# A two-layer streaming encoder on one core: S5 angle multiples from one sine and cosine routine, gate constants ahead of the S5 table, expert gathers at first sizes

## The chip, the cores and the metric

The kernel runs on one core of a Trainium2 chip. The metric is device time in microseconds (us) for one execution. TensorE (PE) multiplies, VectorE (DVE), ScalarE (ACT) and GpSimd (POOL) work on the results, and SyncE (SP) issues most transfers. Each engine runs its own instructions in order and waits on semaphores for the others.

## What is computed

512 frames of 1024 channels go through two layers. Each layer has a token mixer with three branches (chunked attention, RG-LRU, S5) and a channel mixer: a dense SwiGLU in layer 0, eight experts with two chosen per token in layer 1. Cut to what the change touches:

```python
def _rglru_branch(xr, gate, conv_w, conv_b, wx, bx, wa, ba, lam):
    ...
    log_a = -RG_C * ga * jax.nn.softplus(-lam.astype(jnp.float32))
    ...

def _s5_branch(u, a_re, a_im, log_dt, b_re, b_im, c_re, c_im, d, w_glu):
    A = lax.complex(a_re.astype(jnp.float32), a_im.astype(jnp.float32))
    dt = jnp.exp(log_dt.astype(jnp.float32))[:, None]
    A_bar = jnp.exp(A * dt)
    B_bar = ((A_bar - 1.0) / A)[..., None] * Bm
    ...
    states = _linear_scan(A_seq, Bu)

def _moe(x2, router, w1, w3, w2):
    logits = x2.astype(jnp.float32) @ router.astype(jnp.float32)
    top_logit, top_e = lax.top_k(logits, TOP_K)
    ...
    yb = lax.map(expert_block, (xb, blk_e)).reshape(n_pad, dm)
```

## The kernel before

All matrix weights are float32 and are split into two float16 parts (`wh` on ScalarE, `wl` on VectorE, lines L219 and L232); each product is three matmuls (L592 to L594). A unit of weights is 512 KB; it is issued by SyncE into one of eight raw buffers, four units ahead.

**Layer 0, mixer (0 to about 260 us).** The order of the mixer's pieces is a string, `ORDER`, one per layer, written out by hand; each piece issues its instructions on all engines in that order. The pieces that matter: `x.8` and `x.10` are the small S5 parameters (`small_params`, `small_params1`: exponentials, sine and cosine, the factors of B), `x.11` is `a0` (powers of A_bar and B_bar on POOL), `x.13` is `a3` (the table E of 64 powers of A_bar's eighth power, in six doublings, and the radius table R), `x.12` is `rg_params` (the constants of the RG-LRU gates, a softplus of lambda; it ends by writing rgh, L447). All of these run on POOL, one after the other. POOL's list is fed by no planner; it is the order of the string. `small_params` works on both layers at once (16 columns, 8 per layer). Sine and cosine come from `vsincos`; `small_params2` doubles the angle three times by products, and `a3` doubles it five times more in the tile rot.

`ke.0` is the key tile of head pair 0 (kh on ScalarE L1031, kl on VectorE L1033), `z.0` and `z.1` are the RG-LRU gates: `tg` on ScalarE (L698) reads four PSUM banks and rgh, then VectorE continues in tg (L710, L714) with ga (L703) and the scan (L722). `S.0`, `S.1`, ... are the attention scores of one query block (TensorE L866 and L867, then VectorE `sc`, L868, with the running maximum mx, and `nm`, L874); `E.0`, ... the exponentials on ScalarE (L881). PSUM has eight banks. The tiles of S5 and attention share rotating buffers, so a score tile can have to wait until a POOL tile that had its buffer is written or read.

**Dense FFN (to about 640 us).** 22 steps f of 128 hidden columns. A dictionary `z1` hangs layer 1's S5 preparation on single steps: `Z1.steps` (a0, a1, a2, a3, a2s, a4, ...) at f = 1, 2, 3, 4, 8, 9, 11, 12, 14 and `consts` at 18.

**Experts (845 us to the end).** The eight experts are sorted by load and run in four pairs. For each pair and each of up to nine variants in `VARS[p]` (column counts of the two experts) the program holds an arm; a control value read from the router's counts takes one by a chain of branches (`choose`, L1739). Before a pair, `gathers(p, d)` for d = 0 to 7 collects the experts' tokens as products with one-hot matrices (TensorE L1355, 8 matmuls per expert and d), and ScalarE and VectorE write them as float16 parts xg (L1356, L1357). The size of a gather is `TOP`, the largest of the variants: (328, 72), (272, 120), (232, 128), (176, 160). Pair 0's d = 0 to 3 run before the control values are there. Pair 2's gathers stand in two halves around a loop `over` (L1760, L1761) that handles tokens beyond the variants' sizes. In an arm come 22 up steps f of both experts, then eight down steps dt, whose results are copied (`yt`, L1384) and written by `back` (y, L1393). `announce` marks where each engine is told of a coming branch; it stands just ahead of a pair's gathers, and for the loop ahead of pair 2's first half.

## Time and profile before

| | us |
|---|---|
| median of 3 runs | 1708.54 |
| lowest, highest | 1705.78, 1710.72 |
| profiled execution | 1702.69 |
| its span, first to last instruction | 1701.0 |
| TensorE busy in the span | 1606.1 (94%) |
| VectorE busy | 1218.7 (72%) |
| ScalarE busy | 997.1 (59%) |
| POOL busy | 443.2 (26%) |

The mean granted clock of TensorE in the span is 0.965 of its full speed. Shares over the whole span mix stages with different limits, so the table of stretches and the timelines below are read stage by stage. In a timeline, "idle before" is the time in which the engine stood still just before that row, and the name behind the arrow is what ended it.

### The profile page before, as it was taken

What the parts mean: (1) busy time and instruction counts of PE and PEld (TensorE: products, weight loads), DVE (VectorE), ACT (ScalarE), POOL (GpSimd) and SP (SyncE); (2) the same over time, 40 slices, a digit from 0 to 9 for tenths busy, and PEclk for the clock granted to TensorE, in tenths of its full rate; (3) what the DMA queues carried; (4) which work ended last, traced back from release to release, by engine and by line L of the source; (5) the groups of instructions that cost most, each with busy time, mean ns of one, the idle gap of its engine ahead of it and who ended that gap; (6) DMA issues with size and microseconds to landing.
All of it is one profiled execution on the core that took longest, in us unless ns stands there. A gap on an engine that the chain in (4) does not pass through costs nothing. (4 is left out here: it accounts for less than half of the span.)

```text
span 1701.0 us, 44318 instructions
## 1 busy us (share of the span) xinstructions
PE 1606.1 (94%) x18058; PEld 1206.7 (71%) x18058; DVE 1218.7 (72%) x1732; ACT 997.1 (59%) x1643; POOL 443.2 (26%) x643
## 2 busy tenths in 40 slices
PE   8959999999999999899889999999989999999995
PEld 4425555445444444455489999899989999989985
DVE  5856664643342245847779988799978998799987
ACT  5444543232331234645477876788867887678874
POOL 6972015930000000300213321233102331023411
PEclk9978899999999999789899999999999999999998
DMA  7312336322332324210089999799997999899994
GB/s 273 111 38 65 100 100 225 101 98 100 114 125 98 124 69 137 63 50 14 10 320 339 351 341 352 263 381 372 386 360 268 379 363 375 301 328 393 378 383 166
DMA packets 123601, 374.56 MB, mean 220 GB/s; under 512 B 30129, under 2 KB 30321, under 8 KB 123362
## 3 DMA queue, kind: packets, MB, share of 16 engines
q1 hardware_dynamic: 96626, 343.00, 55.0%
q10 hardware_dynamic: 21568, 14.24, 2.8%
q0 software_dynamic: 5168, 14.17, 2.3%
q8 instruction: 146, 2.39, 0.6%
q14 instruction: 93, 0.76, 0.1%
HBM read 356.04 MB, written 14.12 MB: 218 GB/s over the span
## 5 line engine op out<-in xcount | busy, mean ns | idle before, releaser
L594 PEld LDWEIGHTS <-wl 128*128 128x128 f16 x4816 | 463.3, 98 | 96.5 <-DVE wl L232 25.6
L232 DVE SCALAR_TENSOR_TENSOR wl<-raw,wh 128x1024 f16<-128x1024 f32 (+1 forms) x374 | 468.6, 1281 | 76.6 <-PE ps L598 51.4
L592 PEld LDWEIGHTS <-wh 128*128 128x128 f16 x4816 | 463.8, 98 | 69.1 <-issue 4.3
L593 PEld LDWEIGHTS <-wh 128*128 128x128 f16 x4816 | 463.1, 98 | 67.1 <-issue 1.6
L594 PE MATMUL ps<-xg,wl 128*128 128x232 f16 (+7 forms) x2816 | 483.1, 222 | 8.9 <-DVE wl L232 8.4
L592 PE MATMUL ps<-xg,wh 128*128 128x232 f16 (+7 forms) x2816 | 482.9, 222 | 1.4 <-ACT xg L1356 1.1
L593 PE MATMUL ps<-xg,wh 128*128 128x232 f16 (+7 forms) x2816 | 483.5, 222 | 0.0
L219 ACT ACTIVATE wh<-raw 128x1024 f16<-128x1024 f32 (+1 forms) x374 | 376.0, 1031 | 137.3 <-PE ps L599 74.2
L298 POOL TENSOR_TENSOR gbuf<-sg,gbuf 128x232 f16<-128x232 f32 (+7 forms) x176 | 180.1, 1023 | 393.0 <-ACT gbuf L1371 393.0
L594 PE MATMUL ps<-gbuf,wl 128*128 128x232 f16 (+7 forms) x1408 | 246.1, 223 | 10.2 <-DVE wl L232 10.1
L592 PE MATMUL ps<-gbuf,wh 128*128 128x232 f16 (+7 forms) x1408 | 246.4, 223 | 0.0
L593 PE MATMUL ps<-gbuf,wh 128*128 128x232 f16 (+7 forms) x1408 | 246.3, 223 | 0.0
L593 PE MATMUL ps<-fl,wh 128*128 128x512 f16 (+1 forms) x368 | 136.1, 370 | 0.7 <-DVE fl L603 0.7
L592 PE MATMUL ps<-fh,wh 128*128 128x512 f16 (+1 forms) x368 | 136.1, 370 | 0.4 <-ACT fh L602 0.4
L594 PE MATMUL ps<-fh,wl 128*128 128x512 f16 (+1 forms) x368 | 136.1, 370 | 0.0
L1371 ACT ACTIVATE gbuf<-sg 128x232 f16<-128x232 f32 (+7 forms) x176 | 55.4, 315 | 80.7 <-DVE sg L1370 80.7
L286 POOL TENSOR_SCALAR rv<-ss 128x1 f32<-128x1 f32 x24 | 5.1, 214 | 348.1 <-ACT u L609 290.8
L232 DVE SCALAR_TENSOR_TENSOR wl<-raw4m,wh 128x1024 f16<-128x1024 f32 (+1 forms) x68 | 94.8, 1395 | 0.1
L1165 DVE SCALAR_TENSOR_TENSOR slu<-ps,slu 128x512 f32<-128x512 f32 x22 | 15.2, 692 | 109.3 <-PE ps L594 98.4
L232 DVE SCALAR_TENSOR_TENSOR wl<-raw6m,wh 128x1024 f16<-128x1024 f32 (+1 forms) x68 | 87.6, 1289 | 1.8 <-ACT wh L219 1.8
L592 PE MATMUL ps<-uh,wh 128*128 128x512 f16 x224 | 86.5, 386 | 0.0
L593 PE MATMUL ps<-ul,wh 128*128 128x512 f16 x224 | 86.3, 385 | 0.0
(407 smaller groups left out, 2771.8 us busy)
## 6 DMA issues: line engine op xcount, KB each, us to landing
raw<-mw SPq DMA_DIRECT2D x240, 512.0 KB
raw<-fw SPq DMA_DIRECT2D x66, 512.0 KB
raw6m<-mw SPq DMA_DIRECT2D x60, 512.0 KB
raw7m<-mw SPq DMA_DIRECT2D x60, 512.0 KB
raw4m<-mw SPq DMA_DIRECT2D x60, 512.0 KB
raw5m<-mw SPq DMA_DIRECT2D x60, 512.0 KB
raw<-win SPq DMA_DIRECT2D x36, 512.0 KB
raw<-mw SPq DMA_DIRECT2D x32, 384.0 KB
```

Source lines behind the costliest of these rows:

```text
L219: A.activation(whs[u % WH_BUFS][:, :units[u][2]], w_raw(u), AF.Copy, scale=WS)
L232: V.scalar_tensor_tensor(lo, w_raw(u), WS, h, op0=OP.mult, op1=OP.subtract)
L286: P.tensor_scalar(v, ss, inv, EPS, op0=OP.mult, op1=OP.add)
L298: (e or V).tensor_tensor(o, x, y, op=OP.subtract)
L592: T.matmul(ps, wh, xh, start=start, stop=False)
L593: T.matmul(ps, wh, xl, start=False, stop=False)
L594: T.matmul(ps, wl, xh, start=False, stop=stop)
L1165: V.scalar_tensor_tensor(sl, pp[1], OUT_S * GS, sl, op0=OP.mult, op1=OP.mult)
L1371: A.activation(gh[:, f], sg[:, 1, :N], AF.Copy)
```

## The change

Three things. (1) `vsincos` is written anew: it takes the angles as they are, reduces them by whole turns, evaluates the series at a quarter of the angle and doubles twice. It is called once per layer with seven multiples of each angle (1, 8, 16, ..., 256 times; tile `ang`), 8 x 7 = 56 columns, so the doublings in `small_params2` and in rot go; `a3` reads its factors from `ang`. Parameters are per layer: layer 0's in `x.8` and `x.10`, layer 1's at f = 1 and 2 of the dense FFN, and layer 1's preparation starts at f = 3. (2) In layer 0's order `x.12` stands ahead of `x.13`. (3) Gathers ahead of a pair use `VARS[p][0]`, the first variant's sizes; an arm with a larger variant gathers the rest itself (`more`), and the first variant's arm has nothing to add. Pair 2's gathers all come after the loop `over`. The announcements for the loop and for the arms of pairs 1 and 3 move into the pair before, behind down step dt = KD - 3 = 5.

```diff
-    "v.2.0 x.13 A.3 x.12 v.2.1 Ae.3 v.3.0 wb v.3.1 vt.2 vt.3 v.2.2 v.3.2 v.2.3 ve.2 wc v.3.3 v.0.2 v.1.2 v.0.3 v.1.3 ve.3 "
+    "v.2.0 x.12 x.13 A.3 v.2.1 Ae.3 v.3.0 wb v.3.1 vt.2 vt.3 v.2.2 v.3.2 v.2.3 ve.2 wc v.3.3 v.0.2 v.1.2 v.0.3 v.1.3 ve.3 "
...
+    def vsincos(sc, y, n):
+
+        tmp = sm(3 * n, name="sct", bufs=1).rearrange("p (i n) -> p i n", i=3)
+        k, r, t = (tmp[:, i] for i in range(3))
+        P.tensor_scalar(k, y, 0.5 / math.pi, RND, op0=OP.mult, op1=OP.add)
         P.tensor_scalar(k, k, RND, None, op0=OP.subtract)
...
+        for i, c in enumerate((6.28125, 1.9350051879882812e-3, 3.0199159795e-7)):
+            P.tensor_scalar(t, k, -c, None, op0=OP.mult)
+            add(r, t, r if i else y, P)
+        mul(t, r, r, P)
+        r2 = t.unsqueeze(1).to_broadcast([128, 2, n])
+        co = lambda i: srs[:, i].unsqueeze(2).to_broadcast([128, 2, n])
+        mul(sc, r2, co(0), P)
+        for i in range(1, 6):
+            add(sc, sc, co(i), P)
+            if i < 5:
+                mul(sc, sc, r2, P)
         s, c = sc[:, 0], sc[:, 1]
         mul(s, s, r, P)
...
+        for _ in range(2):
+            mul(t, s, s, P)
+            mul(s, s, c, P)
+            add(s, s, s, P)
+            P.tensor_scalar(c, t, -2.0, 1.0, op0=OP.mult, op1=OP.add)
...
-    def small_params2():
         mul(r8, ex, ex, P)
         mul(r8, r8, r8, P)
         mul(r8, r8, r8, P)
-        c, s = cs, sn
-        for i in range(3):
...
         def a3(e=P):
-            if l == 0:
-                small_params2()
...
-            rot = t2([128, 7, 2, 8], name="rot")
-            P.tensor_copy(rot[:, 0, 0], c8[:, j])
-            P.tensor_copy(rot[:, 0, 1], s8[:, j])
-            for i in range(5):
...
             for i in range(6):
                 m = 1 << i
-                br = rot[:, i, 0].unsqueeze(2).to_broadcast([128, 8, m])
-                bi = rot[:, i, 1].unsqueeze(2).to_broadcast([128, 8, m])
+                br = ang[:, 2, i + 1].unsqueeze(2).to_broadcast([128, 8, m])
+                bi = ang[:, 1, i + 1].unsqueeze(2).to_broadcast([128, 8, m])
...
-    z1 = dict(zip((1, 2, 3, 4, 8, 9, 11, 12, 14, 18), Z1.steps + [consts]))
-    z1[2] = lambda: Z1.steps[1](P)
+    z1 = dict(zip((3, 4, 5, 6, 9, 10, 11, 12, 14, 18), Z1.steps + [consts]))
+    z1[1], z1[2] = lambda: small_params(1), lambda: small_params1(1)
+    z1[4] = lambda: Z1.steps[1](P)
...
-        for i in range(2):
-            n = TOP[i * NP_ + p]
-            Expert(n, xgv(p, i, n), None).gather(d, ohv(p, i), low)
+
+        for i, n in enumerate(VARS[p][0]):
+            Expert(n, xgv(p, i, n), None).gather(d, ohv(p, i)[:, :, :n], low)
+
+    def more(p, n):
+
+        for d in range(KD):
+            for i, m in enumerate(VARS[p][0]):
+                if n[i] > m:
+                    x = [t[:, :, m:] for t in xgv(p, i, n[i])]
+                    Expert(n[i] - m, x, None).gather(d, ohv(p, i)[:, :, m:n[i]])
...
+            if dt == KD - 3:
+                announce(None if p == 1 else p + 1)
         back(*last)
...
         if p == 2:
-            announce(n_over > 0, "over")
-            d0 = 4
-            for d in range(d0):
-                gathers(p, d)
             with tc.If(n_over > 0, label="over"):
                 with tc.For_i(0, n_over, 1) as it:
                     beyond(it)
-        announce(ctls[p] > 0, f"pair{p}_0")
-        for d in range(d0, KD):
+        if p % 2 == 0:
+            announce(p)
+        for d in range(4 if p == 0 else 0, KD):
             gathers(p, d, A.copy if p == 0 and d < 6 else V.tensor_copy)
```

The order of instructions, at three places. First POOL in layer 0's mixer, from the end of `a0` (bz) on; pc holds the S5 parameters, Et is scratch of the table E, rgp the gate parameters. Before:

```order
L490 COPY bz<-bb 64x16x16
L292 TENSOR_TENSOR pc<-pc 128x16 [waits Pool_49] x3
L292 TENSOR_TENSOR tv_408<-pc 128x16
...
L423 TENSOR_SCALAR pc<-tv_420 128x16
L521 MEMSET E 128x8
...
L525 COPY rot<-pc 128x8 [waits Pool_49]
...
L292 TENSOR_TENSOR rot<-rot 128x8 [waits Pool_49]
...
L292 TENSOR_TENSOR Et<-E,rot 128x8 x2
...
L540 COPY R<-pc 128x8x63
L431 TENSOR_SCALAR tv_501<-rgp 128x4 [waits DMAHW1_49]
...
L447 TENSOR_SCALAR rgh<-rgp 128x8
```

and now:

```order
L472 COPY bz<-bb 64x16x16
L414 TENSOR_SCALAR tv_387<-rgp 128x4 [waits DMAHW1_49,Pool_49]
...
L326 TENSOR_TENSOR tv_389<-pcn,tv_388 128x4 [waits Pool_49]
...
L429 TENSOR_SCALAR sp_154<-tv_402 128x4
L430 TENSOR_SCALAR rgh<-rgp 128x8
L501 MEMSET E 128x8
...
L292 TENSOR_TENSOR Et<-E,ang 128x8 [waits Pool_49] x2
L298 TENSOR_TENSOR E<-Et 128x8 [waits Pool_49]
...
L512 COPY R<-pc 128x8x63
```

The operations on rgp up to rgh now stand ahead of E, and the products on pc and rot between bz and E are gone.

Second, VectorE from `ke.0` to the gates, where wl is a weight split. Before:

```order
L232 SCALAR_TENSOR_TENSOR wl_116<-raw_104,wh_112 128x1024
L1033 SCALAR_TENSOR_TENSOR kl<-ps,kh 64x512 [waits PE_49,Activation_49,Pool_49]
...
L1035 COPY kh<-kh 64x512 x2
L859 MEMSET bias 64x2x64
L868 ISA sc,mx<-ps,bias 128x128 [waits DVE_49,PE_49,Pool_49]
...
L874 TENSOR_SCALAR nm<-mx 128x2 [waits DVE_49]
L710 SCALAR_TENSOR_TENSOR tg<-tg,xc 128x1024 [waits DMAHW1_49,Activation_49]
L868 ISA sc,mx<-ps,bias 128x256 [waits PE_49]
```

and now:

```order
L232 SCALAR_TENSOR_TENSOR wl_116<-raw_104,wh_112 128x1024
L1005 SCALAR_TENSOR_TENSOR kl<-ps,kh 64x512 [waits PE_49,Activation_49]
...
L1007 COPY kh<-kh 64x512 x2
L831 MEMSET bias 64x2x64
L840 ISA sc,mx<-ps,bias 128x128 [waits DVE_49,PE_49,Pool_49]
...
L846 TENSOR_SCALAR nm<-mx 128x2 [waits DVE_49]
L682 SCALAR_TENSOR_TENSOR tg<-tg,xc 128x1024 [waits DMAHW1_49,Activation_49]
L840 ISA sc,mx<-ps,bias 128x256 [waits PE_49]
```

The order is the same; kl has lost its wait for POOL, the first `sc` keeps one.

Third, ScalarE between pair 1 (yt 128x80 is its last down step's copy) and pair 2 (xg are the gathers). Before:

```order
L219 ACTIVATE wh_108<-raw_100 128x1024 [waits DMAHW7_49,DVE_49]
L1384 ACTIVATE yt<-ps 128x80 [waits PE_49,Activation_49]
L1739 UNCONDITIONAL_BRANCH
...
L1853 BRANCH_PREFETCH_HINT
L1356 ACTIVATE xg_7470<-ps 128x232 [waits PE_49]
L1356 ACTIVATE xg_7470<-ps 128x128 [waits PE_49]
...
L1760 COMPARE_AND_BRANCH
L1761 COMPARE_AND_BRANCH
...
L1853 BRANCH_PREFETCH_HINT
```

and now:

```order
L1834 BRANCH_PREFETCH_HINT
L219 ACTIVATE wh_113<-raw7m 128x768 [waits DMAHW4_49,DVE_49]
...
L1358 ACTIVATE yt<-ps 128x176 [waits PE_49,Activation_49]
...
L1358 ACTIVATE yt<-ps 128x80 [waits PE_49,Activation_49]
L1729 UNCONDITIONAL_BRANCH
L1740 COMPARE_AND_BRANCH
L1741 COMPARE_AND_BRANCH
...
L1834 BRANCH_PREFETCH_HINT
L1330 ACTIVATE xg_7442<-ps 128x160 [waits PE_49]
L1330 ACTIVATE xg_7442<-ps 128x112 [waits PE_49]
```

The hint for the loop (the first BRANCH_PREFETCH_HINT) has moved from behind the arm's last copy to ahead of its last four; the loop's branches (L1760 and L1761, now L1740 and L1741) come before any gather, and the hint for pair 2's arm stands, as before, ahead of gathers, now of all eight.

## Rows read from the trace of the kernel before

**Rows 1.** Stretches, in us: length, busy per engine, granted clock, DMA share, GB/s

```profile
92.00:130.00 38.00, 20.27 (x169) 9.82 (x168) 20.03 (x40) 18.87 (x37) 26.93 (x48) 0.69 0.10 32
...
270.00:500.00 230.00, 230.00 (x1133) 108.99 (x1132) 100.94 (x102) 73.76 (x98) 71.72 (x116) 1.00 0.37 125
...
862.00:1063.00 201.00, 198.00 (x3108) 194.89 (x3107) 178.94 (x214) 152.16 (x237) 51.58 (x50) 1.00 0.93 338
...
1265.00:1290.00 25.00, 20.55 (x265) 19.74 (x266) 11.22 (x25) 9.70 (x24) 2.34 (x3) 0.93 0.37 138
```

**Rows 2.** Instruction groups by form on TensorE: count, busy us, mean ns, idle

```profile
L592 PE MATMUL ps<-xg,wh 128*128 128x232 f16 x352 | 92.4, 262 | 1.1 <-ACT xg L1356 1.1
```

**Rows 3.** Timeline of ScalarE, front: start, length, operation, count, [idle <- releaser]

```profile
92.02 1.19 ACT L1031 ACTIVATE kh<-ps 64x512 f16<-64x512 f32 x2
...
110.19 2.42 ACT L698 ACTIVATE tg<-ps,rgh 128x512 f32<-128x512 f32 x4 [16.98 <-POOL rgh L447]
...
115.35 0.39 ACT L881 ACTIVATE sc<-sc,nm 128x128 f32<-128x128 f32 x1
```

**Rows 4.** Timeline of VectorE, same stretch, columns as above

```profile
98.36 1.39 DVE L1033 SCALAR_TENSOR_TENSOR kl<-ps,kh 64x512 f16<-64x512 f32 x2 [4.52 <-POOL Et L292]
...
100.76 0.29 DVE L868 CUSTOM_DVE_ANT_0 sc<-ps,bias 128x128 f32<-128x128 f32 x1 [0.24 <-POOL tv L298]
...
101.43 0.17 DVE L874 TENSOR_SCALAR nm<-mx 128x2 f32<-128x2 f32 x1
...
111.49 1.22 DVE L710 SCALAR_TENSOR_TENSOR tg<-tg,xc 128x1024 f32<-128x1024 f32 x1 [9.89 <-ACT tg L698]
...
117.73 1.23 DVE L714 SCALAR_TENSOR_TENSOR tg<-xc,tg 128x1024 f32<-128x1024 f32 x1 [2.97 <-ACT tg L707]
```

**Rows 5.** Timeline of TensorE, same stretch

```profile
100.12 0.29 PE L866 MATMUL ps<-kh,q 128*128 128x128 f16 x1 [8.04 <-DVE kh L1035]
...
110.93 0.37 PE L866 MATMUL ps<-kh,q 128*128 128x256 f16 x1 [9.22 <-ACT tg L698]
```

**Rows 6.** Timeline of POOL, 17 to 112 us

```profile
18.67 2.91 POOL L326 TENSOR_TENSOR pc<-pcn,tv 128x16 f32<-128x16 f32 x1
...
56.05 3.58 POOL L292 TENSOR_TENSOR pc<-pc 128x16 f32<-128x16 f32 x3
...
62.12 0.21 POOL L295 TENSOR_TENSOR tv<-tv 128x16 f32<-128x16 f32 x1
...
76.83 1.64 POOL L292 TENSOR_TENSOR Et<-E,rot 128x8 f32<-128x8 f32 x2
...
98.41 0.72 POOL L295 TENSOR_TENSOR E<-Et 128x256 f32<-128x256 f32 x1
...
99.69 0.23 POOL L431 TENSOR_SCALAR tv<-rgp 128x4 f32<-128x4 f32 x1
...
109.92 0.24 POOL L447 TENSOR_SCALAR rgh<-rgp 128x8 f32<-128x8 f32 x1
```

**Rows 7.** Timeline of TensorE: the gathers (L1355) ahead of pairs 0 to 3

```profile
854.35 5.66 PE L1355 MATMUL ps<-ohb,raw 128*128 128x328 f16 x64 [1.34 <-ACT xg L1357]
...
1068.73 10.95 PE L1355 MATMUL ps<-ohb,raw 128*128 128x272 f16 x128
...
1265.68 5.12 PE L1355 MATMUL ps<-ohb,raw 128*128 128x232 f16 x64 [0.32 <-DVE y L1393]
...
1274.88 6.78 PE L1355 MATMUL ps<-ohb,raw 128*128 128x232 f16 x64 [4.07 <-DVEq L1760]
...
1472.10 9.45 PE L1355 MATMUL ps<-ohb,raw 128*128 128x176 f16 x128
```

**Rows 8.** Timeline of ScalarE: the first weight split in pairs 1 to 3

```profile
1082.40 1.06 ACT L219 ACTIVATE wh<-raw 128x1024 f16<-128x1024 f32 x1 [2.41 <-DVE wl L232]
...
1284.40 1.06 ACT L219 ACTIVATE wh<-raw 128x1024 f16<-128x1024 f32 x1 [2.42 <-issue]
...
1484.65 1.06 ACT L219 ACTIVATE wh<-raw 128x1024 f16<-128x1024 f32 x1 [2.77 <-issue]
```

More of the change, by code (lines that the diff above doesn't have):

```diff
@@ L329, in vrcp @@
         P.tensor_tensor(o, x, pcn[:, 2, 0:n], op=OP.pow)
[L331 to L356 removed]
+    q4 = lambda k: (-1.0) ** (k // 2) / math.factorial(k) / 4.0 ** k
@@ new lines, in tile_trunk @@
+    SERIES = [(q4(11 - 2 * i), q4(10 - 2 * i)) for i in range(6)]
+    NM = 7
+    srs = cpool.tile([128, 6, 2], F32, name="srs")
+    mults = cpool.tile([128, NM], F32, name="mults")
+    for i, c in enumerate(SERIES):
+        for k in range(2):
+            P.memset(srs[:, i, k:k + 1], c[k])
+    for i in range(NM):
+        P.memset(mults[:, i:i + 1], 2.0 ** (i + 2 if i else 0))
+    ang = cpool.tile([128, 3, NM, 8], F32, name="ang")
+    def vsincos(sc, y, n):
+        tmp = sm(3 * n, name="sct", bufs=1).rearrange("p (i n) -> p i n", i=3)
+        k, r, t = (tmp[:, i] for i in range(3))
+        P.tensor_scalar(k, y, 0.5 / math.pi, RND, op0=OP.mult, op1=OP.add)
+        P.tensor_scalar(k, k, RND, None, op0=OP.subtract)
+        for i, c in enumerate((6.28125, 1.9350051879882812e-3, 3.0199159795e-7)):
[9 more added lines that the diff above has]
+                mul(sc, sc, r2, P)
@@ L371, in vsincos @@
-        mul(t2_, c, sn_, P)
-        add(so, t1, t2_, P)
-        mul(t1, c, cm, P)
-        mul(t2_, s, sn_, P)
-        sub(co, t1, t2_, P)
-    NP = 16
+        for _ in range(2):
[3 more added lines that the diff above has]
+            P.tensor_scalar(c, t, -2.0, 1.0, op0=OP.mult, op1=OP.add)
     are, aim, ldt = s5p[:, 0], s5p[:, 1], s5p[:, 2]
-    pc = cpool.tile([128, 16, NP], F32, name="pc")
-    dt_, ex, sn, cs, a_re, a_im, f_re, f_im, r8, c8, s8 = (pc[:, i] for i in range(11))
+    pc = cpool.tile([128, 8, 8], F32, name="pc")
@@ L382, in tile_trunk, with small_params @@
+    dt_, ex, a_re, a_im, f_re, f_im, r8, xr = (pc[:, i] for i in range(8))
     sp4 = cpool.tile([128, 2, 2, 2], F32, name="sp4")
     rgh = cpool.tile([128, 2, 2, 2], F32, name="rgh")
-    sp_xr, sp_yi = tv(NP), tv(NP)
-    def small_params():
-        vexp(dt_, ldt, NP)
-        mul(sp_xr, are, dt_, P)
-        mul(sp_yi, aim, dt_, P)
-    def small_params1():
-        vexp(ex, sp_xr, NP)
-        vsincos(sn, cs, sp_yi, NP)
-        mul(a_re, ex, cs, P)
-        mul(a_im, ex, sn, P)
-        m1, t1, t2_, den = tv(NP), tv(NP), tv(NP), tv(NP)
+    def small_params(l=0):
+        j = slice(8 * l, 8 * l + 8)
+        vexp(dt_, ldt[:, j], 8)
+        mul(xr, are[:, j], dt_, P)
+        mul(ang[:, 0, 0], aim[:, j], dt_, P)
+        mul(ang[:, 0, 1:], ang[:, 0, 0:1].to_broadcast([128, NM - 1, 8]), mults[:, 1:].unsqueeze(2).to_broadcast([128, NM - 1, 8]), P)
@@ L398, in small_params1 @@
+    def small_params1(l=0):
+        j = slice(8 * l, 8 * l + 8)
+        re, im = are[:, j], aim[:, j]
+        vexp(ex, xr, 8)
+        vsincos(ang[:, 1:3].rearrange("p i m j -> p i (m j)"), ang[:, 0].rearrange("p m j -> p (m j)"), 8 * NM)
+        mul(a_re, ex, ang[:, 2, 0], P)
+        mul(a_im, ex, ang[:, 1, 0], P)
+        m1, t1, t2_, den = tv(8), tv(8), tv(8), tv(8)
         P.tensor_scalar(m1, a_re, -1.0, None, op0=OP.add)
-        mul(t1, are, are, P)
-        mul(t2_, aim, aim, P)
+        mul(t1, re, re, P)
+        mul(t2_, im, im, P)
@@ L1698, in pair_last, with announce @@
             SY.dma_start(out[b * 128:(b + 1) * 128], of[b])
+    def announce(p):
+        label, c = ("over", n_over) if p is None else (f"pair{p}_0", ctls[p])
+        tc.mark_branch_hint_location(label, c > 0, mybir.ALL_ENGINES)
     def pair(p, v):
@@ L1708, in pair @@
             ex.append(Expert(n[i], xgv(p, i, n[i]), g))
+        more(p, n)
         if p == NP_ - 1:
```

73 lines of the change are left out of this document (10 added, 63 removed).

## The prediction

> **What bounds the kernel now.** I read the table of stretches first [rows 1]. Between 270 and 500 us TensorE is busy for all 230.00 us, so what is added there on other engines costs nothing while it stays beside it. Between 92 and 130 us TensorE works 20.27 of 38.00 us at a granted clock of 0.69: the front of layer 0 waits. From 862 us on the experts run with TensorE busy 198.00 of 201.00 us and the DMA share at 0.93, but in the passage from pair 1 to pair 2 (1265 to 1290 us) that share is 0.37 and VectorE works 11.22 of 25.00 us. So two places have slack in which a shorter chain is a shorter program: the front and the passages between pairs. The forms of the up matmuls [rows 2] name the variant taken: 352 matmuls at 232 columns are pair 0's smallest variant, (232, 56), and the other forms (56, 176, 80, 160, 112, 136, 120) are the first variants of the other three. The gathers, however, run at the largest sizes (328 and 72 for pair 0).
>
> Then the three timelines of the front. ScalarE, done with kh at 93.21, stands 16.98 us until POOL's rgh, and runs `tg` at 110.19 [rows 3]. POOL ends rgh at 110.16, after the rotation table E (last write 98.41 + 0.72 = 99.13) and after the 34 operations of the gate constants from 99.69 on [rows 6]. VectorE and TensorE stand behind ScalarE: the first tg on VectorE is at 111.49 after 9.89 us idle [rows 4], the second pair of S matmuls at 110.93 after 9.22 us, since `tg` holds the banks [rows 5]. Before that VectorE's kl waited 4.52 us for a late read of POOL's scratch tile Et [rows 4].
>
> **The change, part 1: the front.** It moves the gate constants (x.12) ahead of the table (x.13), removes the doubling chain of `small_params2` (12 operations) and the rotation chain (22), and computes sine and cosine of seven angle multiples at once, on 8 columns per layer: operations of 56 and 112 columns instead of 16 and 32. The rows of the order show that kl loses its POOL wait, that S.0's first `sc` on VectorE keeps one (the write of E ends just ahead of it in the trace, and I take that to be it), and that `tg` waits only for rgh.
>
> POOL's new chain: its exponentials start at 18.67 as before. The 128x16 form took 2.91 us [rows 6]; on 8 columns I estimate 1.7. Replaying the new list with the durations of the old rows, and letting an operation that starts beside a VectorE operation on SBUF last until that ends (the three products at 56.05 took 1.19 each, the sum at 62.12 took 0.21 [rows 6]), a0 ends at about 55.8 as now, since more columns per operation eat what fewer operations save. The 34 operations of the constants then fall into the stretch where VectorE is busiest: about 23 us instead of the 10.5 of 99.69 to 110.16. So rgh comes at about 79 (77 to 82) instead of 110.16, 14 us before ScalarE can use it. E starts at about 79, 2 us later than today's first product of it (76.83 [rows 6]); of that the replay gives back some, as fewer of its operations lie beside VectorE's, and E ends at about 99, as now (97 to 102).
>
> What is late next: ScalarE runs `tg` at 93.2, 17 us earlier. VectorE does kl right after its weight split, near 94, and then S.0's `sc` waits for the end of E, about 99, instead of 100.76. From the `sc` row to the tg row behind it lie four short rows, the last of which ends at 101.60 [rows 4], 0.84 us in all, so tg comes at 99.85 instead of 111.49: 11.6 us. The 2.97 us that VectorE idles at 117.73 for ScalarE [rows 4] go as well, since ScalarE's `sc` of 115.35 [rows 3] then stands 15 us earlier and the sigmoid behind it no longer ends last; then the gain is up to 14.6. The U matmuls, in order behind S.3, set which of the two counts. I take 13. Bounds: 9.6 (E at 101, no more) to 16 (E at 97, and a clock that falls less, 0.69 in this stretch [rows 1]). Behind it the layer's order is a fixed chain on three engines, and it passes the gain on.
>
> Layer 1's parameters move into the dense FFN, some 24 us of POOL operations in its steps 1 and 2, and layer 1's preparation two steps later. TensorE is the bound there [rows 1]; POOL has 71.72 of 230.00 us in use and VectorE 100.94. Nothing, and below nothing there is no reason. If this cover were gone it would be at most those 24 us.
>
> **Part 2: the gathers.** Columns per d and term fall: 400 to 288, 392 to 256, 360 to 272, 336 to 256. A d has 8 passes over these columns. The passage from pair 0 to 1 took 10.95 us for 8 x 8 x 392 columns, 0.44 ns each [rows 7], and the others lie within 2% of that.
> - Pair 0: only d 4 to 7 stand on the path (5.66 us; d 0 to 3 end before a wait that ends later). 4 x 8 x 288 columns take 4.05: 1.6 us.
> - Pair 1: 8 x 8 x 256 columns take 7.15 instead of 10.95: 3.8 us.
> - Pair 3: 7.15 instead of 9.45: 2.3 us.
> - Pair 2: today 5.12 us of gathers, 4.07 idle until VectorE has its branch, 6.78 for the other half (1.66 more than the first; the stretch's granted clock is 0.93 [rows 1], and I put the difference down to a clock that fell after the idle), and ScalarE's split at 1284.40, 2.74 later [rows 7, 8]: 18.7 in all. After the change the branch comes first: 4.07 + 7.7 (272 columns) + 1.66 + 2.74 = 16.2, a gain of 2.5. If the idle shortens because the branch was announced two down steps earlier, or the clock holds, it is up to 8. I take 4.
>
> Together 11.7. It isn't eaten by the weights' transfer: a passage leaves DMA idle (0.37 of 25 us [rows 1]) because the raw buffers are full; a passage that ends earlier starts the queue earlier.
>
> The announcements for pairs 1 and 3 and for the overflow loop move behind the third down step from the end. Before, with the announcement ahead of the whole gather, ScalarE's first split in the arm still came after 2.41, 2.42 and 2.77 us of idle [rows 8]. ScalarE's announcement for pair 1 stood some 11 us ahead of the branch and the 2.41 came all the same, so I expect nothing from more distance: 0, with 2.5 us per passage either way.
> The Trainium skill, "Runtime: NRT & Kernel Launch", section "Instruction fetch mechanics", says that prefetch is sequential over two pages of 256 instructions, and that a taken branch to a target outside them stalls for a fetch. By it an announcement made hundreds of TensorE instructions ahead could be thrown out again before the branch; the sum would then lose the first rival's price. No row of before shows an announcement that far ahead.
>
> **The sum.** 13 + 1.6 + 3.8 + 4 + 2.3 = 24.7 us. The profiled execution took 1702.69 (span 1701.0), which would become 1678.0. It lies 5.85 us under the median of the runs, 1708.54, so the predicted median is 1683.8, say 1684. A measurement of this kernel can tell about 0.3%, 5 us, from no change.
>
> **The rivals.**
> 1. *The early announcement is lost.* Three branches (pair 1, overflow, pair 3) then pay a fetch that today is announced: 2.77 (ScalarE's longest start) to 4.07 us (TensorE's wait for VectorE at a branch) each, 8 to 12 in all: 1692 to 1696. For it: between announcement and branch now lie two down steps of both experts and the jump at the arm's end, where before there was one gather. Against it: after a passage TensorE stands about 2.7 us ahead of ScalarE's split anyway [rows 7, 8], so TensorE's own fetch would partly hide, and ScalarE's start was no better with the announcement close by. Chance 0.14.
> 2. *E comes late and gates S.0.* If all 34 operations of the constants took 1.19 us, as those at 56.05, they would last 40 us and not 23, E would end at 115, tg on VectorE at 116: 4.5 us lost instead of 13 won, 1701. Halfway, E at 107, the front gains 3.5: 1693. Against it: not every operation there is stretched (0.21 at 62.12 [rows 6]), and VectorE's work on SBUF ends near 94, before kl. Chance 0.12.
> 3. *The weights set the experts' time.* With a DMA share of 0.93 the savings of part 2 would be given back in the next pair: 1708.5 - 13 = 1695. Against it: the idle DMA of each passage. Chance 0.06.
> 4. *Slower: announcements fetch twice.* At the same three places an early announcement costs a stall where its page comes in and another fetch at the branch. At 4.07 each, twice three times, 24 us are lost and the change is worth nothing; above that it is slower, and by over 0.3% from 5 us each, 30 in all: 1714. It would need more than the longest such wait in the trace, which a DMA queue near its limit (0.93) could cause. Chance 0.03.
> 5. *Better:* the announced branches save 2.5 us at three passages, or the front brings 16: 1668 to 1675. Chance 0.03.
>
> **How the numbers follow.** The forecast has 0.62, on its own 1676 to 1691. The range that leaves out no more than 2 in 10 takes in the first three rivals' middles: 1674 to 1699. Faster by over 0.3%, under 1703.4: the forecast, rivals 1, 2, 3 and 5, less a little of 2's far end: 0.93. Within 0.3%: 0.04. Slower: 0.03.
>
> **What would show it.** In the front: rgh near 79, `tg` on ScalarE near 93, no POOL wait ahead of kl, S.0's `sc` right behind the last write of E near 99, tg on VectorE near 100. In the passages: gathers of pairs 1 and 3 near 7.2 us and ScalarE's first split 2.4 to 2.8 us after the last eviction; pair 2's gathers in one piece behind the overflow branch. The dense FFN as long as before. Wrong would be: E after 103, idle TensorE inside a down step of pairs 0, 1 or 2, or a pair that takes longer from its first split to its last than before.

## The result

The changed kernel takes 1688.53 us (median of 4 runs, 1683.74 to 1691.41) against 1709.63 for the kernel before: a ratio of 0.9893, 95% interval 0.9870 to 0.9916. In a second comparison on another chip it was 1689.89 against 1705.35, 0.9903 (0.9880 to 0.9926). So the gain is 16.5 to 18.3 us by the ratios (15.5 and 21.1 by the medians, whose quotients differ a little from the ratios), where 24.7 was forecast. The time lies 4.5 us above the predicted 1684, inside the range.

The front in the changed kernel first. Columns of a timeline: start, length, engine and line, operation, tiles, count, idle time before and what ended it. POOL:

```profile
79.59 0.74 POOL L430 TENSOR_SCALAR rgh<-rgp 128x8 f32<-128x8 f32 x1
...
102.17 1.89 POOL L292 TENSOR_TENSOR xc<-ga 128x1024 f32<-128x1024 f32 x1 [1.47 <-DVE tg L682]
104.00 3.54 POOL L550 MEMSET wt<- 128x2048 f16 x2
```

ScalarE and VectorE:

```profile
92.56 2.42 ACT L670 ACTIVATE tg<-ps,rgh 128x512 f32<-128x512 f32 x4
...
107.87 0.62 ACT L853 ACTIVATE sc<-sc,nm 128x384 f32<-128x384 f32 x1 [4.62 <-DVE nm L846]
```

```profile
93.04 1.39 DVE L1005 SCALAR_TENSOR_TENSOR kl<-ps,kh 64x512 f16<-64x512 f32 x2
...
100.15 0.29 DVE L840 CUSTOM_DVE_ANT_0 sc<-ps,bias 128x128 f32<-128x128 f32 x1 [4.82 <-POOL E L295]
...
100.77 1.23 DVE L682 SCALAR_TENSOR_TENSOR tg<-tg,xc 128x1024 f32<-128x1024 f32 x1
...
102.72 4.85 DVE L846 TENSOR_SCALAR nm<-mx 128x2 f32<-128x2 f32 x1
104.00 3.57 DVE L840 CUSTOM_DVE_ANT_0 sc<-ps,bias 128x384 f32<-128x384 f32 x1
...
110.30 2.48 DVE L292 TENSOR_TENSOR dm<-ps,E 128x512 f32<-128x512 f32 x4
```

Four things stand in these rows. rgh ends at 80.33 and no longer holds `tg`, which starts at 92.56 [against rows 3]. kl has no wait [rows 4]. The first score waits 4.82 us for the table E, as forecast. And a wait that was not forecast stands behind them: nm, an operation on 256 numbers, lasts 4.85 us, and the score behind it 3.57; both end at 107.57, with POOL's zeroing of `wt`.

The experts, in stretches cut at the same events in both kernels: first gather, first up result (`sg`) of a pair, last copy (`yt`) of its down steps. Columns: stretch, length, busy time (instructions) of PE, PEld, DVE, ACT and POOL, granted clock, DMA share, GB/s. The changed kernel, into pair 0, 0 to 1, 1 to 2, 2 to 3, and pair 3 with its DMA share of 0.90:

```profile
834.87:856.09 21.22, 16.56 (x178) 14.54 (x178) 10.64 (x47) 12.75 (x36) 0.00 (x0) 0.85 0.69 253
...
1056.38:1069.25 12.87, 12.57 (x214) 12.29 (x215) 6.80 (x21) 6.33 (x20) 1.86 (x2) 1.00 0.52 196
...
1249.66:1268.51 18.85, 13.18 (x184) 12.93 (x185) 7.54 (x21) 6.76 (x20) 1.32 (x2) 0.91 0.37 140
...
1455.05:1466.30 11.25, 10.64 (x183) 10.49 (x184) 5.47 (x19) 6.68 (x21) 1.20 (x2) 1.00 0.68 255
1466.30:1674.52 208.22, 191.76 (x3201) 186.93 (x3198) 192.41 (x234) 153.18 (x254) 57.25 (x52) 0.97 0.90 328
```

The same stretches for all kernels, in us, one profiled execution each ("to g0" is the time of the first gather):

| kernel | to g0 | into 0 | pair 0 | 0 to 1 | pair 1 | 1 to 2 | pair 2 | 2 to 3 | pair 3 |
|---|---|---|---|---|---|---|---|---|---|
| before | 845.9 | 20.2 | 202.2 | 16.0 | 180.5 | 21.5 | 185.3 | 15.0 | 200.8 |
| changed | 834.9 | 21.2 | 200.3 | 12.9 | 180.4 | 18.9 | 186.5 | 11.2 | 208.2 |
| e11, changed again | 831.3 | 22.0 | 200.3 | 13.3 | 182.2 | 18.9 | 186.5 | 12.0 | 208.2 |
| e1, front alone | 832.7 | 20.0 | 203.7 | 18.4 | 180.0 | 21.8 | 185.3 | 15.0 | 200.5 |
| e2, gathers alone | 850.7 | 21.4 | 200.1 | 12.4 | 180.7 | 19.4 | 186.5 | 12.4 | 204.2 |
| e3, table first | 834.6 | 22.2 | 200.4 | 12.8 | 181.7 | 19.2 | 186.8 | 11.2 | 205.7 |
| e4, zeroing late | 836.4 | 21.9 | 201.3 | 14.1 | 183.9 | 19.0 | 186.2 | 12.6 | 202.3 |
| e12, zeroing late again | 838.0 | 22.3 | 198.6 | 13.0 | 179.8 | 19.4 | 186.4 | 11.9 | 205.8 |
| e5, gathers twice | 835.0 | 20.9 | 200.5 | 20.0 | 179.6 | 27.4 | 186.4 | 18.0 | 202.0 |
| e6, announced late | 834.1 | 21.2 | 200.3 | 13.4 | 180.7 | 22.3 | 186.3 | 13.0 | 202.5 |
| e9, pair 0 wide | 834.2 | 21.3 | 200.3 | 12.1 | 182.1 | 19.8 | 186.4 | 13.0 | 199.3 |
| e10, order alone | 840.6 | 20.0 | 202.9 | 16.1 | 179.4 | 21.7 | 185.9 | 15.0 | 202.0 |
| e7, changed, half transfers | 836.1 | 22.5 | 198.6 | 12.7 | 179.7 | 16.5 | 186.3 | 11.1 | 197.1 |
| e8, before, half transfers | 844.7 | 20.0 | 202.6 | 17.0 | 179.1 | 21.9 | 185.0 | 15.1 | 196.5 |

A single execution carries a spread that the columns show: 831 to 836 up to the first gather for one and the same front (changed, e11, e1, e5, e6, e9, e7), 199 to 208 for pair 3 with the same gathers ahead of it. Means over the rows of a kind are compared below, and where the rows of two kinds overlap the text says so.

The first up result is not all that a pair's start waits for: the up steps need VectorE's splits as well. Counted to the first result of the third up step (f = 2) instead, the passages 0 to 1, 1 to 2 and 2 to 3 take 21.5 to 23.9, 27.6 to 27.7 and 20.7 to 20.9 us with the old gathers (before, e1, e10), 18.7 to 20.2, 24.8 to 26.0 and 18.7 to 19.3 with the new ones (changed, e11, e2, e3, e4, e12, e9), and 19.3, 27.8 and 18.6 in e6.

### The profile page after: what moved, and what is told of

It reads as the page before. It is cut to its first block, busy times and chain, and to the rows that moved or that the text cites. A ratio compares the mean times of both kernels' runs of the same rounds, so it can differ in the third digit from the quotient of the medians.

```text
span 1688.0 us, 44316 instructions
## 1 busy us (share of the span) xinstructions
PE 1603.4 (95%) x18058; PEld 1204.1 (71%) x18058; DVE 1219.4 (72%) x1732; ACT 994.1 (59%) x1643; POOL 454.2 (27%) x636
## 5 line engine op out<-in xcount | busy, mean ns | idle before, releaser
L298 POOL TENSOR_TENSOR gbuf<-sg,gbuf 128x232 f16<-128x232 f32 (+7 forms) x176 | 180.2, 1024 | 386.1 <-ACT gbuf L1345 359.7
L566 PE MATMUL ps<-gbuf,wl 128*128 128x232 f16 (+7 forms) x1408 | 249.0, 225 | 11.6 <-DVE wl L232 11.5
L564 PE MATMUL ps<-gbuf,wh 128*128 128x232 f16 (+7 forms) x1408 | 249.4, 225 | 0.0
L565 PE MATMUL ps<-gbuf,wh 128*128 128x232 f16 (+7 forms) x1408 | 249.2, 225 | 0.0
```

The source lines that it names most:

```text
L298: (e or V).tensor_tensor(o, x, y, op=OP.subtract)
L564: T.matmul(ps, wh, xh, start=start, stop=False)
L565: T.matmul(ps, wh, xl, start=False, stop=False)
L566: T.matmul(ps, wl, xh, start=False, stop=stop)
```

## The experiments

### The two halves of the change (e1, e2)

e1 is the kernel before with the new sine and cosine routine, the parameters per layer and the order; e2 is the kernel before with the gathers and announcements. The cut in the diff runs ahead of the class of experts, all hunks above in e1, all below in e2.

> The front of the change alone (new sine and cosine routine, parameters per layer, gate constants ahead of the table); gathers and announcements as before. Additive theory: the passages keep their old lengths and the program is 9 to 11 us faster than before, what the two profiles show up to the first gather (845.92 against 834.87). Weight-stream theory (a shorter passage is given back where the weights end last): the front lies ahead of the experts' stream, so it is the same 9 to 11 us here, and the rest of the change is worth less than the 9.7 us that its three passages lost (3.2, 2.7 and 3.7).

> The gathers and the announcements of the change alone on the kernel before; front as before. Additive theory: 9 to 10 us faster than before. Weight-stream theory: 3 to 7 us, with the first split of pair 3 still 9 us earlier and its end no more than 3 to 6 us earlier, since in the profile of the changed kernel pair 3 gave back 7.5 us behind its passage.

Measured: e1 0.9927 (0.9904 to 0.9950), 12.5 us faster; e2 0.9951 (0.9929 to 0.9973), 8.4 us faster. Together 20.9, against 16.5 to 18.3 for the whole: additive within the intervals. e1 is 1.5 us over the 9 to 11 that both theories expected. e2 is 0.6 us short of the additive theory and 1.4 over the other, and its interval, 4.6 to 12 us, does not tell the two apart. In its profile, counted from the first gather, pair 3 begins 7.9 us earlier than before and ends 4.4 earlier, near what the second theory had (9, and 3 to 6), in one execution of each.

### Chains or order (e3, e10)

e3 puts the table ahead of the gate constants in the changed kernel; e10 puts the constants ahead of the table in the kernel before.

```diff
-    "v.2.0 x.12 x.13 A.3 v.2.1 Ae.3 v.3.0 wb v.3.1 vt.2 vt.3 v.2.2 v.3.2 v.2.3 ve.2 wc v.3.3 v.0.2 v.1.2 v.0.3 v.1.3 ve.3 "
+    "v.2.0 x.13 A.3 x.12 v.2.1 Ae.3 v.3.0 wb v.3.1 vt.2 vt.3 v.2.2 v.3.2 v.2.3 ve.2 wc v.3.3 v.0.2 v.1.2 v.0.3 v.1.3 ve.3 "
```

> The changed kernel with one word of the order put back: the table (x.13) ahead of the gate constants (x.12). If the order is what gains, rgh comes late again and the front loses part of its 10 us. If the removed chains are what gains: the table ends near 82, the constants, in a stretch in which VectorE does less, near 93 to 95, tg on ScalarE starts at 93 to 95, and the first score on VectorE no longer waits 4.82 us for the table: near 96. Then the front is 1 to 4 us faster than the changed kernel.

> The kernel before with the order alone changed: gate constants ahead of the table, old sine and cosine, old chains. rgh near 79 and tg on ScalarE near 93; the doubling and rotation chains and the table follow, 43 us long as before, so the table ends near 116 to 122 and the first score on VectorE waits for it. If the chains' removal is what gains and the order is worth nothing by itself, this kernel is 4 to 11 us slower than before. If the order gains, 8 us or more faster.

e3: 1687.75, ratio 0.9893 (0.9841 to 0.9944), the changed kernel's within an interval of some 9 us either way. R, behind the table, starts at 85.23, but the constants, in contention with VectorE, end at 99.71 and not at 93 to 95, so `tg` waits and dm on VectorE starts at 109.85 (changed: 110.30):

```profile
99.75 1.84 ACT L670 ACTIVATE tg<-ps,rgh 128x512 f32<-128x512 f32 x3 [4.66 <-POOL rgh L430]
```

```profile
107.29 1.23 DVE L686 SCALAR_TENSOR_TENSOR tg<-xc,tg 128x1024 f32<-128x1024 f32 x1 [2.97 <-ACT tg L679]
```

e10: 0.9987 (0.9965 to 1.0008), no change that its interval shows (the medians lie 4.5 us apart); the expected loss of 4 to 11 us did not come. `tg` starts at 92.21, but kl and the first score wait for the old chains, and dm starts at 120.20, to 0.1 us where it was before:

```profile
107.53 1.39 DVE L1033 SCALAR_TENSOR_TENSOR kl<-ps,kh 64x512 f16<-64x512 f32 x2 [15.00 <-POOL Et L292]
109.92 0.29 DVE L868 CUSTOM_DVE_ANT_0 sc<-ps,bias 128x128 f32<-128x128 f32 x1 [0.24 <-PE ps L867]
...
112.62 4.85 DVE L874 TENSOR_SCALAR nm<-mx 128x2 f32<-128x2 f32 x1
```

Both orders give the same time with the old chains, and both with the new, as far as the intervals tell. What gains is that the later of table and constants ends 8 to 10 us earlier without the chains: R starts at 108.28 in e10 and at 100.10 in the changed kernel, rgh ends at 110.16 before [rows 6] and at 99.71 in e3.

That the two orders are equal has a second reason, which the rows of nm show. With the constants first (changed, e10) nm lasts 4.85 us. With the table first (before, e3) it does not, and VectorE stands 2.97 us for ScalarE instead. Each order pays a wait of its own. With the zeroing of the next section moved away, dm starts at 107.91 and 107.79, 2 us ahead of e3's 109.85: on the new chains the new order is then the better one by the profiles. The old chains with the new order and the zeroing moved were not run.

### The zeroing on POOL (e4, e12)

```diff
-    "ke.0 z.0 z.1 S.0 ra rx E.0 rt b.1 S.1 S.2 rb E.2 x.4 E.1 rr S.3 s1 E.3 rs q.1 qe.1 T.0 T.1 D.0 k.1 ke.1 V.0 f1 T.2 D.1 "
+    "ke.0 z.0 z.1 S.0 ra rx E.0 rt b.1 S.1 S.2 rb E.2 E.1 rr S.3 s1 E.3 rs x.4 q.1 qe.1 T.0 T.1 D.0 k.1 ke.1 V.0 f1 T.2 D.1 "
```

> The changed kernel with POOL's zeroing of the two wt tiles (3.54 us at 104.00) moved behind the gates. If this zeroing holds up VectorE (nm took 4.85 us at 102.72 and ended with it, at 107.57), nm is 0.2 to 1.5 us long, dm on VectorE starts near 106 instead of 110.30, and the program is 2 to 4.5 us faster than the changed kernel. If the stall is something else (TensorE's fetch at 104.02, a wait for PSUM), nm and the scores behind it stay 3 to 5 us long.

> The changed kernel with the zeroing of wt behind the gates, against the changed kernel on the same chip: 2 to 3 us faster, what dm on VectorE gained (10.2 us behind R in the changed kernel, 7.6 with the late zeroing).

In the kernel before, POOL's zeroing and VectorE's nm at that time:

```profile
117.36 3.55 POOL L578 MEMSET wt<- 128x2048 f16 x2
```

```profile
120.21 0.72 DVE L874 TENSOR_SCALAR nm<-mx 128x2 f32<-128x2 f32 x1
```

VectorE in e4:

```profile
100.98 1.23 DVE L682 SCALAR_TENSOR_TENSOR tg<-tg,xc 128x1024 f32<-128x1024 f32 x1
...
102.92 1.37 DVE L846 TENSOR_SCALAR nm<-mx 128x2 f32<-128x2 f32 x1
104.21 0.55 DVE L840 CUSTOM_DVE_ANT_0 sc<-ps,bias 128x384 f32<-128x384 f32 x1
...
107.91 2.48 DVE L292 TENSOR_TENSOR dm<-ps,E 128x512 f32<-128x512 f32 x4
```

nm is down from 4.85 to 1.37 us (in e12 too) and the score behind it from 3.57 to 0.55: the zeroing is shown to be what held both. dm starts at 107.91 (near 106 was expected), 7.6 us behind R's start (100.31) and not 10.2, so 2.6 us are won there. In times, e12 is 1687.93 and the changed kernel beside it 1689.89, 2.0 us, with intervals that overlap (0.9864 to 0.9913 and 0.9880 to 0.9926); e4, on the chip of e1 to e3, was 0.9872 beside e3's 0.9893. It is the best version that was run, and by times alone it is not told from the changed kernel.

The rest of nm's 1.37 us is POOL's product on xc (1.89 us from 102.25 in e12). The Trainium skill, "SBUF — State Buffer", section "SBUF: two separate sides", describes the port pair that VectorE and GpSimd share as an exclusive lock that the loser waits for in full. The trace agrees, and the wait went on over more than one instruction: nm began beside the product and in the changed kernel came back only when the product and both zeroings, which stand back to back, were done (107.57); in e4 and e12, without the zeroings, it came back with the product.

### The passage into pair 0 (e9, and e11)

```diff
-        for i, n in enumerate(VARS[p][0]):
+        for i, n in enumerate(VARS[p][0] if p else (TOP[0], TOP[NP_])):
```

> The changed kernel with pair 0's gathers at the old sizes (328 and 72), the others at the first sizes. In the changed kernel the passage into pair 0 took 21.2 to 22.5 us from the first gather to the first up result, before 20.0 to 20.2, though it has fewer columns. If a lower clock after a longer idle is the cause (granted clock 0.83 and 0.75 in the two stretches of 4 us, before 1.00), the wide gathers bring back 20.0 to 20.3 us and a clock of 1.00 there, and pair 0 is 202 us again; the sum is the same within 1 us. If the sizes gain what was forecast, the passage is 1.6 us longer than 21.2.

> The changed kernel once more, on the chip of the runs beside it, for a second profile. Pair 3 took 208.2 us in its first profile and 202.0 to 205.7 in five kernels with the same experts; expected 202 to 206, and the program 16 to 21 us faster than before.

e9 takes 21.3 us into pair 0: the wide gathers do not bring back 20.0, so neither expectation holds (the clock beside its gathers is 1.00, as expected). Its time, 1687.89 us (0.9895), is the changed kernel's. e11's second profile gives pair 3 208.2 us again, over the 202 to 206 expected; its gain, 16.5 us by the ratio, lies inside the 16 to 21. It also shows why the sizes do not count on the way into pair 0. TensorE, ScalarE and VectorE:

```profile
839.73 4.17 PE L1329 MATMUL ps<-ohb,raw 128*128 128x232 f16 x64 [2.74 <-ACT wh L219]
...
846.68 0.26 PE L564 MATMUL ps<-xg,wh 128*128 128x232 f16 x1 [2.79 <-issue]
```

```profile
846.69 2.00 ACT L219 ACTIVATE wh<-raw 128x1024 f16<-128x1024 f32 x2 [2.49 <-issue]
```

```profile
851.31 2.36 DVE L232 SCALAR_TENSOR_TENSOR wl<-raw,wh 128x1024 f16<-128x1024 f32 x2 [6.67 <-ACT wh L219]
```

The kernel before at the same place, VectorE and TensorE:

```profile
866.13 1.22 DVE L232 SCALAR_TENSOR_TENSOR wl<-raw,wh 128x1024 f16<-128x1024 f32 x1 [5.59 <-ACT wh L219]
```

```profile
867.41 0.20 PE L594 MATMUL ps<-xg,wl 128*128 128x56 f16 x1 [1.29 <-DVE wl L232]
```

e11's gathers d 4 to 7 take 4.17 us, what the forecast had (4.05), against 5.66 [rows 7]. In the first profile of the changed kernel they took 5.80, beside a clock of 0.83 and 0.75:

```profile
843.31 5.80 PE L1329 MATMUL ps<-ohb,raw 128*128 128x232 f16 x64 [2.81 <-ACT wh L219]
```

In four of the nine profiles with narrow gathers they end as late as the wide ones. But TensorE starts no earlier in the arm in any. Counted from the control values, which VectorE writes last (ctl, ended at 838.42 in e11 and 853.03 before), the arm's first matmul on TensorE comes 8.26 us later (before 8.10) and VectorE's first split 12.89 (before 13.10). In all 13 kernels of which this was read these are 7.9 to 8.8 and 12.1 to 13.6 us, whether the gathers ended 5.5 or 7.1 us behind the control values (with the new expert part VectorE has 12.1 to 13.3 in the first case and 13.3 to 13.6 in the second). So what ends last there is the branch, from control value to arm, and VectorE comes out of it last: before, TensorE stood 1.29 us for that split.

The first up result itself comes later with the new expert part: 13.8 to 15.4 us behind the control values in ten profiles, e9's 14.2 among them, against 12.9 to 13.1 in the four with the old one (before, e1, e8, e10). Part of it is the clock. Where the gathers end early, TensorE waits longer for the branch, and in four of five such profiles the clock falls behind that wait. e11, the wait and a stretch behind it:

```profile
843.90:846.68 2.78, 0.00 (x1) 0.10 (x1) 0.52 (x2) 0.29 (x2) 0.00 (x0) 1.00 1.02 371
848.00:851.20 3.20, 3.20 (x19) 2.46 (x17) 0.00 (x0) 3.20 (x4) 0.00 (x0) 0.50 0.27 88
```

The granted clock is 0.50, the level of 1.2 GHz, for the first up matmuls: 19 of 232 columns in 3.20 us. The clock is not all of it. In e2 and e9 it stays at 1.00 there, and the first result comes 14.3 and 14.2 us behind the control values all the same: TensorE begins the arm 0.4 us or more later than with the old expert part and stops once more inside the first up step, which it does not do there. e9:

```profile
853.70 0.27 PE L566 MATMUL ps<-xg,wl 128*128 128x232 f16 x1 [0.43 <-issue]
```

What ends this stop the profile does not name. The front (e2 has the old one), the announcements (e6 has the old ones) and the sizes (e9) are not its cause, which stays open. Passage and pair 0 together take 222.4 to 223.7 us with the old expert part (before, e1, e10), 220.9 to 223.2 with the new one (changed, e11, e2, e3, e4, e12) and 221.6 in e9 with the wide gathers. The rows overlap, and no gain by the narrow gathers is shown here.

### The announcements (e6)

```diff
-            if dt == KD - 3:
-                announce(None if p == 1 else p + 1)
...
         if p == 2:
+            announce(None)
             with tc.If(n_over > 0, label="over"):
...
-        if p % 2 == 0:
-            announce(p)
+        announce(p)
```

> The changed kernel with the announcements back where they stood: just ahead of the gathers for pairs 1 and 3, just ahead of the overflow loop's branch for the loop. If early announcements cost nothing: the same time within noise, and the first splits and matmuls in the arms start as late as now. If they are lost on the way: TensorE's first matmul of pair 3 starts 0.5 to 2 us earlier (it began 0.01 to 1.4 us after the last eviction with the change and 0.5 us before it without), ScalarE's first split of pair 3 comes at 2.8 us instead of 0.7, and the whole is within 4 us of the changed kernel either way. If they help: pair 2's gathers start later than 4.8 us after the last copy of pair 1.

1690.80 us, 0.9932 (0.9909 to 0.9955), against 0.9893 and 0.9903 for the changed kernel: 5 to 7 us slower by the ratios and 1 to 2 by the medians, with intervals that overlap. The profiles tell more. TensorE's gathers ahead of pair 2, in the changed kernel and in e6:

```profile
1254.47 9.23 PE L1329 MATMUL ps<-ohb,raw 128*128 128x160 f16 x128 [4.23 <-ACTq L1740]
```

```profile
1257.11 9.26 PE L1329 MATMUL ps<-ohb,raw 128*128 128x160 f16 x128 [6.75 <-PEq L1739]
```

The loop's branch costs TensorE 4.23 us of idle with the early announcement and 6.75 without, and the gathers start 7.1 us behind the last copy, as the third expectation had it. The passage 1 to 2 takes 22.3 us in e6 and 18.9 to 19.8 in the seven profiles with the early announcement. The passages 0 to 1 and 2 to 3, 13.4 and 13.0 us, lie within the others' rows (12.1 to 14.1 and 11.2 to 13.0).

In the passage to pair 3 ScalarE gains. Its first split in the changed kernel and in e6:

```profile
1463.89 1.06 ACT L219 ACTIVATE wh<-raw 128x1024 f16<-128x1024 f32 x1 [0.70 <-DVE xg L1331]
```

```profile
1469.47 1.06 ACT L219 ACTIVATE wh<-raw 128x1024 f16<-128x1024 f32 x1 [2.89 <-issue]
```

So it was expected; e9, which announces early too, has 2.95. VectorE, whose split the up step needs as well, does not gain. Its first split in the changed kernel and in e6:

```profile
1466.65 2.36 DVE L232 SCALAR_TENSOR_TENSOR wl<-raw,wh 128x1024 f16<-128x1024 f32 x2 [3.14 <-DMA gfin<-final_norm_g]
```

```profile
1469.61 2.36 DVE L232 SCALAR_TENSOR_TENSOR wl<-raw,wh 128x1024 f16<-128x1024 f32 x2 [2.72 <-issue]
```

These come 11.6 and 11.2 us behind the last copy, and counted to the third up step the passage takes 18.6 us in e6 against 18.7 to 19.3. So the early announcement helps at the loop's branch, where TensorE's idle is 2.5 us shorter; for the arms of pairs 1 and 3 no gain of time is shown.

### The stream of weights (e5, e7, e8)

e5 does the gathers ahead of pairs 1 to 3 a second time. e7 and e8 bring half of the columns of each unit of expert weights.

```diff
             gathers(p, d, A.copy if p == 0 and d < 6 else V.tensor_copy)
+        if p > 0:
+            for d in range(KD):
+                gathers(p, d)
```

```diff
+            if W.n_dma >= W.half:
+                n = n // 2
-            SY.dma_start(w_raw(W.n_dma), src(o, n) if callable(src) else src[:, o:o + n])
+            SY.dma_start(w_raw(W.n_dma)[:, :n], src(o, n) if callable(src) else src[:, o:o + n])
```

> The changed kernel with the gathers ahead of pairs 1, 2 and 3 done a second time (the same products once more): each passage 7.1 to 7.6 us longer, 22 us in all. Additive theory: 22 us slower than the changed kernel, near 1710. Weight-stream theory (the stream of weights is what ends last in pairs 2 and 3, so a longer passage is partly made up behind it, as a shorter one was given back): the three passages are 22 us longer in the profile and pairs 1 to 3 together 4 to 10 us shorter, so 12 to 18 us slower.

> The changed kernel in which each transfer of expert weights, from the 17th on, brings half of the columns (the other half of the raw buffer keeps what it held, so the products are others). Weight-stream theory: without a full stream the passages' gain is not given back; pairs 1 to 3 take as long here as in the kernel before with the same halving, within 1 us each, and the halved pair of kernels differs by the whole 19 to 22 us. Additive theory: the same, with the full-stream kernels differing by as much. Pair 3 alone falls from 208 us to 195 to 203.

> The kernel before with the same halving of the expert weights' transfers (products are others). Weight-stream theory: pair 3 is 195 to 200 us, as long as in the changed kernel halved, where with the full stream it was 200.8 against 202 to 208. If pair 3 stays longer in the changed kernel halved too, the stream is not the cause.

e5: 1.0029 (1.0011 to 1.0046), 1707.1 us, which is 17 to 19 us over the changed kernel's medians, or 21 to 23 by the ratios; its profile is 15 us longer. The three passages are 22.4 us longer than in the first profile of the changed kernel, and pairs 1 to 3 together 7 us shorter than there, 0.9 of it in pairs 1 and 2 and the rest in pair 3, whose 202.0 lies within the changed kernel's spread. Times and profile point to different sides of the two expectations, so e5 is inconclusive.

e7 and e8: 1677.85 and 1697.02, ratios 0.9862 and 0.9962, so 17 to 19 us apart, where the weight-stream theory had the whole 19 to 22; with the full stream it is 16.5 to 18.3 by the ratios. By times, then, a full stream is not seen to take anything back. Pair 3 with the full stream, before and changed (e11):

```profile
1486.56:1687.32 200.76, 186.62 (x3176) 182.47 (x3174) 190.53 (x233) 153.52 (x255) 55.16 (x52) 0.98 0.91 340
```

```profile
1466.50:1674.66 208.16, 191.09 (x3201) 186.41 (x3198) 192.40 (x234) 153.24 (x254) 57.26 (x52) 0.97 0.90 327
```

e7 (changed) and e8 (before), pair 3 with the halved stream:

```profile
1463.49:1660.64 197.15, 186.17 (x3201) 182.56 (x3198) 191.97 (x234) 151.47 (x254) 55.27 (x52) 0.99 0.61 185
```

```profile
1485.51:1681.98 196.47, 184.86 (x3173) 181.08 (x3171) 190.26 (x233) 151.44 (x255) 57.21 (x52) 0.99 0.59 186
```

With the halved stream (DMA share 0.61 and 0.59) pair 3 is the same length within 0.7 us in both, as e8's expectation had it; pair 2 is 1.3 us longer in the changed one, over the 1 us that e7's allowed. With the full stream (0.90) pair 3 is 201.1 on average with the old gathers (before, e1, e10: 200.5 to 202.0) and 204.8 with the new (the changed kernel twice, e2, e3, e4, e9, e12: 199.3 to 208.2). So the full stream lengthens pair 3 by some 5 us with the old gathers and, in rows that overlap with these, some 8 with the new. The chain of waits of the changed kernel shows where; columns: start, length, what:

```profile
1499.91 6.98 DMA raw6m<-mw
...
1535.61 8.39 DMA raw<-mw
...
1550.89 6.96 DMA raw<-mw
...
1572.91 7.37 DMA raw<-mw
```

These four transfers stand on the chain in the up steps of pair 3; in the chain of the kernel before the up steps have one such piece. In the other profiles whose chain runs through these steps their number goes roughly with pair 3's length: four in e11 (208.2), three in e2 (204.2), two in e3 (205.7) and e1 (200.5), one in e12 (205.8), e6 (202.5) and e10 (202.0), none in e9 (199.3), e7 and e8. That a full stream lengthens pair 3 is shown by the halving. That it takes back part of the passages' gain is suggested by the means (3.7 us) and by the chains and is not shown: the rows overlap, and the halved kernels lie no further apart than the full ones.

## Why the prediction was right or wrong

The time and the sign were right, and the front and the passages to pairs 1 to 3 gained in the way that was forecast; the sum was 6 to 8 us too large by the ratios. Three of its steps failed: the last part of the front's term, the path into pair 0, and the nothing for pairs 1 to 3. That the time came within 4.5 us of the forecast, and not 6 to 8, owes something to the medians that were compared. Means over the table's rows of a kind (old gathers: before, e1, e10; new: the seven named above; front: first gather in eight kernels with the new front, 834.1, against before, e2 and e8, 847.1, or 845.5 with e10, whose old chains gave the same dm):

| term | forecast | measured |
|---|---|---|
| front | 13 | 13.0 up to the first gather (11.4 with e10); 10.0 at dm in the first profile |
| pair 0 | 1.6 | 1.1 (passage 1.7 longer, pair 0 2.7 shorter), rows overlap |
| passage to pair 1 | 3.8 | 3.9 |
| passage to pair 2 | 4 | 2.4 |
| passage to pair 3 | 2.3 | 3.0 |
| pairs 1 to 3 | 0 | -6.3 (1.6, 1.0 and 3.7 longer; the first and the last in rows that overlap) |
| sum | 24.7 | 17.1 (15.5 with e10) |

**The front.** POOL's replay held: rgh 80.3 for 79, the end of E 100.1 for 99, tg on VectorE 100.77 for 99.85. The bound that counted was the end of E, as the text said, and its lower value, 11.6, was nearer: 10.7 at tg. The step that failed is the one behind it, "the 2.97 us that VectorE idles ... go as well": ahead of that place a new wait of 4.6 us came up, nm behind POOL's product and zeroing. Before, the zeroing ran later beside VectorE and cost 0.55 us (nm at 120.21, 0.72 us long). The replay had moved POOL's list and looked at who delays POOL, not at whom POOL delays. That the gain up to the first gather is 11 to 13 all the same, and 12.5 by e1's runs, is partly luck with the layers behind: the rows with old chains lie at 840.6 to 850.7 there, those with new ones at 831.3 to 836.1 (838.0 with the zeroing late). In the first profile layer 1's gates ran their matmuls at the higher clock and gained 1.6 us that the change did not touch.

The removed chains are what gains. The order by itself brought nothing (e3, e10), because with the constants first the wait at nm came in its place. The text gave no separate term for the order.

**Pair 0.** "Only d 4 to 7 stand on the path" is the step that failed. The gathers shortened as computed where the clock held (4.17 for 4.05 in e11), but the branch, some 8 us behind the control values on TensorE and 13 on VectorE, ends last, and with the wide gathers (e9) passage and pair take no longer. The trace of the kernel before told it, in a row that the prediction did not read: VectorE idles 5.59 us there. The text took the gathers for the path because they were the busy rows.

**The passages.** Pair 1 was right (3.9; 3.2 counted to the third up step). For pair 2 the working gave 2.5 and the text took 4 for an idle that might shorten; it did not (4.23 for 4.07), so the working's own figure was the better one. Pair 3 came out above its term, 3.0, but counted to the third up step it is 1.8: the early announcement brought ScalarE's split forward (0.70 us for 2.89) and not VectorE's. The step "0" for the announcements held in time for pairs 1 and 3, though not as argued, for ScalarE's first split in pair 3 came after 0.70 us and not 2.4 to 2.8. At the loop's branch it was wrong: without the early announcement (e6) the passage to pair 2, with the gathers now all behind that branch, would have gained nothing (22.3 for 21.5). So rival 1, and with it the fourth, fall. The Trainium skill, "Runtime: NRT & Kernel Launch", section "Instruction fetch mechanics", speaks of a sequential prefetch and of a stall at a taken branch outside the window, and the text drew from it that an announcement hundreds of TensorE instructions ahead could be lost. The same section of the Trainium skill gives TensorE room for 2048 instructions, four times that of most engines, which the text left out. Here two down steps of matmuls and a jump lie between, and TensorE still waits 2.5 us less: the trace does not bear that use of the rule out.

**Pairs 1 to 3.** The step that failed is the one that keeps the passages' gains whole, argued from the idle DMA of the passages. By the means 6.3 of 9.3 us are missing behind the passages. First, 1.8 of these were never won: counted to the third up step the passages gained 7.5 and not 9.3, and in pair 3 of the changed kernel VectorE's first split, at 1466.65, now begins behind the first up result, at 1466.30. Second, behind that step pair 2 is 1.0 us longer in every row, in e6 and with the halved stream too (180.2 against 179.2), so neither the announcements nor the stream is the cause, which was not followed; one of the text's own signs of being wrong, a pair that takes longer than before, thus came up. Third, pairs 1 and 3 are 0.9 and 2.6 us longer there, in rows that overlap. For pair 3 this is what rival 3 has, the weights, and e7 and e8 fit it by the lengths of pair 3 and not by their times. That the idle of a passage is where the next pair's reserve of weights is filled would explain it; no run shows that.
